# Operand b22 at the beginning of the FFN: when its high and low parts are made

## The chip, the core and the metric

The kernel runs on one core of a Trainium2 chip. Five engines work side by side and meet at semaphores: TensorE (PE, with its weight loads shown as PEld), VectorE (DVE), ScalarE (ACT), GpSimd (POOL) and SyncE (SP), which here issues nearly all DMAs. The metric is device time in microseconds for one execution of the whole block; the time of a kernel is the median of its runs.

## The reference

One decoder block on x (1 x 2048 x 1024): a mixer of eight stick-breaking attention heads and four pooling groups, and then a SwiGLU FFN of width 2816. Both have an RMSNorm ahead and behind, and are modulated from a vector c. What matters here is the passage from the mixer to the FFN:

```python
mix = jnp.concatenate([attn, pool], axis=-1) @ w_out[l]
x = x + gate_m * rmsnorm(mix, g_mix_post[l])

h = rmsnorm(x, g_ffn_pre[l]) * (1.0 + scale_f) + shift_f
f = (jax.nn.silu(h @ w_gate[l]) * (h @ w_up[l])) @ w_down[l]
x = x + gate_f * rmsnorm(f, g_ffn_post[l])
```

All is float32.

## The kernel before

**Products of float32.** Each operand of a product is split into a high part, rounded to the format that TensorE multiplies (a cast on ScalarE, line 59), and a low part, the rest (a subtraction on VectorE, line 60, which reads the source and the high part). `mm3` (lines 69 to 71) then makes three matmuls: high by high, low by high, high by low. `put(ops, n, cols, src)` (line 1156) is this split for 128 columns of a named operand.

**The FFN's products.** The 2048 tokens are taken in two halves of 1024. In each half the gate and up products are made as 2 x 2 block products with seven multiplications instead of eight. The token side has seven operands, b11, b21, t2, t3, t1, t4 and b22, sums and differences of quarters of h transposed (128 partitions x 4 x 512, a high and a low tile each). The weight side has a11, a12, s2, s3, s1, a22 and s4, made for each pair of 128-column blocks of a weight matrix by sums on GpSimd (lines 1267 to 1278). One *step* is one such product: four chunks of the inner dimension times three matmuls, twelve matmuls of 128x128 by 128x512, into one PSUM bank. For the first block of weights (j = 0 of the first half) the steps of the gate (g) and of the up matrix (u) are interleaved by `gate_up`:

- steps 0, 1: g with b11, b21; steps 2, 3: u with b11, b21
- steps 4, 5: g with t2, t3; steps 6, 7: u with t2, t3
- steps 8, 9, 10: g with t1, t4, b22; steps 11, 12, 13: u with t1, t4, b22
- from step 14 on: the next block of weights, seven g steps and then seven u steps

**PSUM.** Banks come from `f_ps` (line 1031), a cycle of eight tags with one buffer each. A step takes one, and so does each half of a row that is transposed (`modulated_t`, the tile `f_pt`). Results leave their bank by the functions a step has in `take`, which run one step later: `take_p1` copies it on ScalarE (line 1287), `plus` adds it to an earlier one on VectorE (line 1282, tiles `u2`, `u3`, `u4`), and `take_gate` adds it and applies Silu (lines 1331, 1332).

**The order around the beginning of the FFN.** The order of TensorE, ScalarE, VectorE and GpSimd is the order of the calls in the program. SP's is made by the compiler's planner: a DMA is put in when its tile's slot is free. The main loop (from line 1801) does for each step n: the functions due ahead of it, the step's matmuls, `end_of_rows(n)`, `split_up_to(n)` (which splits the weights up to five steps ahead), and then the takes due and a piece of a side job. At the beginning of the FFN three things stand beside the steps:

- the last row block of the mixer (its 128 tokens, `SEQUENCE[-1]`): `add_last_x` (line 1207) adds x in `split_up_to(0)`, `ffn_rows` (line 1193) squares and sums it on ScalarE after the step 0, `end_of_rows(1)` scales it (`x1s`, lines 1201 and 1202), and `put_h2` transposes, modulates and stores it;
- the late operands. t1, t4 and b22 have their room only once the mixer's tiles are closed. Their raw rows lie in DRAM and are loaded by `load` (line 1410) into twelve slots borrowed from other tags (`tr`, `gs`, `u4`, `s`); b22 takes the four slots of `tr`. All twelve loads are issued before step 0;
- `puts` (line 1413), a generator, splits them: one stretch between two `yield`s with each call of `next_side`.

Before the change `puts` runs through this list, where a number is one `put` (0 to 3 are the columns of b22, 4 to 7 of t1, 8 to 11 of t4) and None is the end of a stretch:

```python
for m in (0, 1, None, None, 4, 5, 6, 7, None, 8, 9, 10, 11, None, 2, 3, None):
```

So b22's first two columns are split in step 0, t1 in step 2, t4 in step 3, b22's other two columns in step 4, and the last row is put in step 5. In step 2 the side job runs ahead of the takes (the first gate sum, step 1's), in the others behind them.

Of the kernel before, what the change touches and what calls it, by code (L numbers as in the profile page):

```python
# [12 lines left out]
ALU = mybir.AluOpType  # L13
# [4 lines left out]
P = 128  # L18
# [3 lines left out]
HK = KC // 2  # L22
# [22 lines left out]
def block_kernel(ctx, tc, x, c, w_cond, b_cond, g_mix_pre, g_mix_post, w_in, w_pool,  # L45
                 pool_scale, w_out, g_ffn_pre, g_ffn_post, w_gate, w_up, w_down, out):
    nc = tc.nc
# [6 lines left out]
    def raw(ap):  # L54
        return ap.bitcast(F32)

    def split(hi, lo, src, low=nc.vector):

        nc.scalar.copy(hi, src)  # L59
        low.tensor_tensor(lo, src, raw(hi), ALU.subtract)  # L60
# [12 lines left out]
    def open_pool(stack, name, bufs=1, side=None):  # L73
        kw = {"side": side} if side else {}
        return stack.enter_context(tc.tile_pool(name=name, bufs=bufs, reuse_waits="tile", **kw))
# [39 lines left out]
    def ft(tag, name, shape=(P, TB)):  # L115
        return fx.tile(list(shape), F32, tag=tag, bufs=FT[tag], name=name)

    def rstd_of(pool, ss, name):

        v = pool.tile([P, 1], F32, tag="rs_v", bufs=2, name=f"{name}_v")  # L120
        nc.vector.tensor_scalar(v, ss, 1.0 / D, EPS, ALU.mult, ALU.add)
        r = pool.tile([P, 1], F32, tag="rs_r", bufs=4, name=f"{name}_r")
        nc.gpsimd.tensor_tensor(r, v, mhalf, ALU.pow)
        return r
# [174 lines left out]
    def normed_rows(tb, j, xs=None):  # L299
        t0 = tb * TB + j * P  # L300
        xt = tokp.tile([P, D], F32, tag="xt", name=f"xt{tb}_{j}")
        ss = tokp.tile([P, 1], F32, tag="ss", name=f"ss{tb}_{j}")
        if xs is None:
            xs = tokp.tile([P, D], F32, tag="xs", name=f"xs{tb}_{j}")
            nc.sync.dma_start(xt, xf[t0:t0 + P, :])
            nc.scalar.activation(xs, xt, AF.Square, scale=1.0 / 32, accum_out=ss)
        else:
            nc.scalar.activation(xt, xs, AF.Square, scale=1.0 / 32, accum_out=ss)
            xt = xs
        r = tokp.tile([P, 1], F32, tag="rs_r", bufs=4, name=f"x{tb}_{j}_r")  # L310
        v = tokp.tile([P, 1], F32, tag="rs_v", bufs=2, name=f"x{tb}_{j}_v")
        nc.vector.tensor_scalar(v, ss, 1.0, EPS, ALU.mult, ALU.add)
        nc.gpsimd.tensor_tensor(r, v, mhalf, ALU.pow)
        if tb == 1:
            return lambda: nc.vector.tensor_scalar_mul(xs, xt, r)
        nc.vector.tensor_scalar_mul(xs, xt, r)
        return xs
# [240 lines left out]
    loaded = []  # L558
# [144 lines left out]
    last_scale = normed_rows(1, 3, early1[3])  # L703
# [325 lines left out]
    SEQUENCE = [sb * NT // 2 + half * 4 + i for sb in range(2) for i in range(4) for half in range(2)]  # L1029
# [55 lines left out]
    for n in range(len(steps) + OFF):  # L1085
# [4 lines left out]
        if n < len(steps):  # L1090
            u, i = steps[n]
# [19 lines left out]
        for pool, here in ((hb, not wo and taken >= HB_FREE), (ha, len(wo) == 4 and fill is None)):  # L1111
            if here:
                hi, lo = (pool.tile([P, 4, D], F32R, tag=tag, name=f"wo_{pool.name}{tag}")
                          for tag in ("hi", "lo"))
# [32 lines left out]
    def new_ops(pool, sb, names):  # L1147
        return {n: (pool.tile([P, HK, TB], F32R, tag=f"{n}h", bufs=1, name=f"{n}h{sb}"),
                    pool.tile([P, HK, TB], F32R, tag=f"{n}l", bufs=1, name=f"{n}l{sb}")) for n in names}
# [6 lines left out]
    def put(ops, n, cols, src, low=nc.vector):  # L1156
        split(ops[n][0][:, :, cols], ops[n][1][:, :, cols], src, low)

    h2st, b22st = ExitStack(), ExitStack()
    ops = new_ops(open_pool(h2st, "ops0"), 0, EARLY)  # L1160
# [6 lines left out]
    def after_mix(T):  # L1167

        pss = mixed.pop(T)
        if T == SEQUENCE[-1]:  # L1170
            xt = last_x[0]
        else:
            xt = op.tile([P, D], F32, tag="xt", name=f"xr{T}")
            nc.sync.dma_start(xt, xf[T * P:(T + 1) * P, :])
        ss = op.tile([P, 2], F32, tag="ss", name=f"mss{T}")
        x1 = op.tile([P, D], F32, tag="x1", name=f"x1_{T}")
        halves = [slice(nh * TB, (nh + 1) * TB) for nh in range(2)]
        for nh in range(2):
            nc.scalar.activation(x1[:, halves[nh]], pss[nh], AF.Square, accum_out=ss[:, nh:nh + 1])
        nc.vector.tensor_tensor(ss[:, 0:1], ss[:, 0:1], ss[:, 1:2], ALU.add)  # L1180
        r = rstd_of(op, ss[:, 0:1], f"mr{T}")
        for nh in range(2):
            nc.vector.scalar_tensor_tensor(x1[:, halves[nh]], pss[nh], r, gm[:, halves[nh]], ALU.mult, ALU.mult)
            if T != SEQUENCE[-1]:
                nc.gpsimd.tensor_tensor(x1[:, halves[nh]], x1[:, halves[nh]], xt[:, halves[nh]], ALU.add)
        if T != SEQUENCE[-1]:
            nc.sync.dma_start(x1d[T], x1)
        return xt, x1

    def ffn_rows(T, xt, x1):  # L1190

        s2 = op.tile([P, 1], F32, tag="s2", name=f"s2_{T}")
        nc.scalar.activation(xt, x1, AF.Square, accum_out=s2)
        r2 = rstd_of(op, s2, f"fr{T}")
        if T != SEQUENCE[-1]:
            nc.vector.tensor_scalar_mul(xt, x1, r2)
            return xt

        def scale():
            xs = ft("gf", f"x1s{T}", (P, D))  # L1200
            nc.vector.tensor_scalar_mul(xs[:, 0:TB], x1[:, 0:TB], r2)
            nc.scalar.mul(xs[:, TB:], x1[:, TB:], r2)
            return xs
        return scale
# [7 lines left out]
    def put_h2(T, xs, pool=None):  # L1212

        i, second = T % NTS % HK, T % NTS >= HK
        cols = slice(i * P, (i + 1) * P)
        for kcs, h32 in modulated_t(pool or op, f_ps, xs, mods["af"], mods["bf"], f"f{T}"):
            nc.sync.dma_start(h2d[T][:, kcs, :], h32)
            if T >= NTS:
                continue
            low_k = kcs.start == 0  # L1220
            if not second:
                n = "b11" if low_k else "b21"
                put(ops, n, cols, h32)
                held_rows[n] = h32
            elif low_k:
                held_rows["b12"] = h32
            else:
                t3, t2 = held_rows["b12"], held_rows["b11"]
                nc.vector.tensor_tensor(t3, h32, t3, ALU.subtract)
                put(ops, "t3", cols, t3)  # L1230
                nc.vector.tensor_tensor(t2, t3, t2, ALU.add)
                put(ops, "t2", cols, t2)
                for n, t in (("t1", h32), ("t4", held_rows["b21"])):
                    nc.gpsimd.tensor_tensor(t, t, t2, ALU.subtract)
                    nc.sync.dma_start(lated[n][i], t)
# [164 lines left out]
    def late_operands():  # L1400

        slots = ["tr"] * 4 + ["gs"] * 3 + ["u4"] + ["s"] * 4
        todo = [(n, i) for n in ("b22", "t1", "t4") for i in range(HK)]
        raw = []

        def load():
            if len(raw) < len(todo):
                n, i = todo[len(raw)]
                t = ft(slots[len(raw) % len(slots)], f"{n}{i}_raw", (P, HK, P))
                nc.sync.dma_start(t, lated[n][i] if n in lated else h2d[HK + i][:, HK:KC, :])  # L1410
                raw.append(t)

        def puts():
            for m in (0, 1, None, None, 4, 5, 6, 7, None, 8, 9, 10, 11, None, 2, 3, None):
                if m is None:
                    yield
                    continue
                n, i = todo[m]
                put(ops, n, slice(i * P, (i + 1) * P), raw[m])
            put_h2(*late.pop(0), fx)  # L1420
            yield

        for _ in slots:
            load()
        return puts
# [348 lines left out]
    last_rows, last_scale = after_mix(SEQUENCE[-1]), []  # L1774
# [10 lines left out]
    takes, side, slow = {}, None, []  # L1785
# [3 lines left out]
    def next_side():  # L1789

        nonlocal side
        if slow:
            if next(slow[0], 0) == 0:
                slow.pop()
        elif side is not None and (n < HF or n % 2) and next(side, 0) == 0:
            side = None

    for n, s in enumerate(steps):
        for do in ahead.get(n, []):
            do()  # L1800
        s.ps = s.mm()
        end_of_rows(n)
        split_up_to(n)
        if n == 0:
            last_scale.append(ffn_rows(SEQUENCE[-1], *last_rows))
        if n in sides:
            side = sides[n]()
        jobs = [lambda: [do() for do in takes.pop(n, [])], lambda: next_side()]
        for do in jobs[::-1] if n == 2 else jobs:
            do()  # L1810
        for k, do in s.take:
            takes.setdefault(n + k, []).append(do)
    for n in sorted(takes):
# [28 lines left out]
```

## Time and profile before

| what | value |
|---|---|
| time, median of 3 runs | 2255.8 us (2254.81 to 2256.67) |
| profiled execution, its own time | 2258.0 us |
| its span, first to last instruction | 2256.2 us |
| mean granted TensorE clock | 0.998 |
| TensorE busy | 2231.4 us (99%) |
| VectorE busy | 1624.0 us (72%) |
| ScalarE busy | 1166.6 us (52%) |
| GpSimd busy | 1273.2 us (56%) |

All rows come from one profiled execution, with times in us from the first instruction. A row of the timeline is: start, duration, engine, source line, operation, output <- inputs, shape and count; several instructions of one kind in sequence are merged into one row (x2, x4), whose duration goes from the first start to the last end. In brackets stands how long the engine was idle ahead of it and what it waited for, as inferred from semaphore events. Matmuls are pipelined: one is shown with 0.39 us, but the next starts 0.227 us later, so a step's length is read from starts. Line 59 is the high part of any operand and line 60 the low part; the names tell which (`g_s_h` is the high part of a gate weight sum, `g_a_h` of a gate quarter, `b22l` the low part of b22).

### The profile page before, as it was taken

What the parts mean: (1) busy time and instruction counts of PE and PEld (TensorE: products, weight loads), DVE (VectorE), ACT (ScalarE), POOL (GpSimd) and SP (SyncE); (2) the same over time, 40 slices, a digit from 0 to 9 for tenths busy, and PEclk for the clock granted to TensorE, in tenths of its full rate; (3) what the DMA queues carried; (4) which work ended last, traced back from release to release, by engine and by line L of the source; (5) the groups of instructions that cost most, each with busy time, mean ns of one, the idle gap of its engine ahead of it and who ended that gap; (6) DMA issues with size and microseconds to landing.
All of it is one profiled execution on the core that took longest, in us unless ns stands there. A gap on an engine that the chain in (4) does not pass through costs nothing.

```text
span 2256.2 us, 33256 instructions
## 1 busy us (share of the span) xinstructions
PE 2231.4 (99%) x10613; PEld 1845.8 (82%) x10613; DVE 1624.0 (72%) x2227; ACT 1166.6 (52%) x2425; POOL 1273.2 (56%) x1579
## 2 busy tenths in 40 slices
PE   8999999999999999999999999999999999999998
PEld 6888888888888888888888888788888888888887
DVE  7874599999999957666565656777866555655566
ACT  5435599898999944452232323455532323234444
POOL 1452277787779955546868687321677565651003
PEclk9999999999999999999999999999999999999999
DMA  9986876534443556665554545777853333328664
GB/s 316 338 278 213 283 203 182 153 107 114 123 121 104 164 179 218 219 212 162 159 164 159 164 159 195 266 234 239 259 169 122 94 117 94 112 89 293 219 188 149
DMA packets 323980, 413.55 MB, mean 183 GB/s; under 512 B 20630, under 2 KB 189146, under 8 KB 323676
## 3 DMA queue, kind: packets, MB, share of 16 engines
q1 hardware_dynamic: 319196, 408.81, 57.1%
q10 hardware_dynamic: 4608, 2.63, 0.4%
q8 instruction: 83, 1.36, 0.3%
q14 instruction: 93, 0.76, 0.1%
HBM read 282.90 MB, written 128.45 MB: 182 GB/s over the span
## 4 chain that ended last, share of the span: by engine, by line
PE 87%; DVE 6%; ACT 2%; POOL 2%; issue 2%; DMA 1%; SPq 0%; DVEq 0%; ACTq 0%; POOLq 0%
PE wt L961 4%; PE t_u L70 3%; PE t_u L69 3%; PE t_u L71 3%; PE t_g L70 3%; PE t_g L69 3%; PE t_g L71 3%; PE dn0p L70 3%; PE dn0p L71 3%; PE dn0p L69 3%; PE dn1p L70 3%; PE dn1p L69 3%; PE dn1p L71 3%; PE mix L71 3%; PE mix L69 3%; PE mix L70 3%
## 5 line engine op out<-in xcount | busy, mean ns | idle before, releaser
L950 POOL TENSOR_TENSOR w<-sg,pr 128x512 f32<-128x512 f32 (+2 forms) x320 | 307.2, 960 | 46.5 <-DVE pr L945 13.4
L1342 POOL TENSOR_TENSOR s<-s,cu 128x512 f32<-128x512 f32 x88 | 133.9, 1528 | 240.3 <-DVE cu L1341 145.8
L945 DVE TENSOR_TENSOR_SCAN pr<-pr,carry,begin 128x512 f32<-128x512 f32 x192 | 243.9, 1271 | 0.0
L929 ACT ACTIVATE sg<-z 128x512 f32<-128x512 f32 (+2 forms) x320 | 183.4, 573 | 50.8 <-PE z L927 40.4
L60 DVE TENSOR_TENSOR wtl<-wt,wth 128x512 fp32r<-128x512 f32 (+1 forms) x320 | 189.3, 592 | 18.0 <-ACT wth L59 15.9
L59 ACT CAST wth<-wt 128x512 fp32r<-128x512 f32 (+1 forms) x320 | 182.1, 570 | 12.1 <-PE wt L961 12.1
L931 ACT ACTIVATE pr<-z 128x512 f32<-128x512 f32 (+2 forms) x320 | 182.5, 570 | 0.0
L961 PE MATMUL wt<-ident,w 128*128 128x128 f32 x1088 | 172.6, 273 | 2.0 <-POOL pr L941 1.1
L60 DVE TENSOR_TENSOR u_s_l<-u_s,u_s_h 128x512 fp32r<-128x512 f32 x66 | 65.2, 987 | 150.1 <-ACT u_s_h L59 150.0
L961 PEld LDWEIGHTS wt<-ident,w 128*128 128x128 f32 x1088 | 134.1, 140 | 33.4 <-POOL pr L941 1.9
L1332 ACT ACTIVATE s<-s 128x512 f32<-128x512 f32 x88 | 55.7, 633 | 190.5 <-DVE s L1331 190.5
L976 PE MATMUL av<-wth,vt 128*128 128x512 f32 (+1 forms) x320 | 126.5, 395 | 0.9 <-ACT o L981 0.8
L60 DVE TENSOR_TENSOR u_a_l<-u,u_a_h 128x512 fp32r<-128x512 f32 x66 | 77.1, 1169 | 63.7 <-ACT u_a_h L59 63.7
L70 PE MATMUL dn0p<-w0p_l,g0p_h 128*128 128x512 f32 x308 | 120.3, 391 | 1.0 <-DVE w0p_l L60 1.0
L59 ACT CAST g_s_h<-g_s 128x512 fp32r<-128x512 f32 x66 | 39.5, 620 | 157.8 <-POOL g_s L1274 78.2
L977 PE MATMUL av<-wtl,vt 128*128 128x512 f32 (+1 forms) x320 | 118.0, 369 | 1.9 <-DVE wtl L60 1.6
L69 PE MATMUL dn0p<-w0p_h,g0p_h 128*128 128x512 f32 x308 | 119.8, 389 | 0.0
L71 PE MATMUL dn0p<-w0p_h,g0p_l 128*128 128x512 f32 x308 | 119.8, 389 | 0.0
L926 PE MATMUL z<-kt,qt 128*128 128x512 f32 (+2 forms) x320 | 118.7, 371 | 0.7 <-ACT pr L931 0.6
L927 PE MATMUL z<-kt,qt 128*128 128x512 f32 (+2 forms) x320 | 117.0, 366 | 0.0
L59 ACT CAST u_s_h<-u_s 128x512 fp32r<-128x512 f32 x66 | 38.6, 614 | 150.3 <-POOL u_s L1274 149.1
L69 PE MATMUL dn1p<-w1p_h,g1p_h 128*128 128x512 f32 x292 | 113.6, 389 | 0.0
(657 smaller groups left out, 7184.2 us busy)
## 6 DMA issues: line engine op xcount, KB each, us to landing
g<-in_w_gate_dram SPq DMA_DIRECT2D x42, 512.0 KB, 5.3
u<-in_w_up_dram SPq DMA_DIRECT2D x42, 512.0 KB, 4.2
wc<-in_w_cond_dram SPq DMA_DIRECT2D x32, 512.0 KB, 7.5
qt<-qd SPq DMA_DIRECT2D x64, 256.0 KB, 4.0
kt<-kd SPq DMA_DIRECT2D x96, 128.0 KB, 3.3
vt<-vd SPq DMA_DIRECT2D x48, 256.0 KB, 4.0
wd<-in_w_down_dram SPq DMA_DIRECT2D x44, 256.0 KB, 3.4
tdt<-wd SPq DMA_DIRECT2D x44, 256.0 KB, 2.0
```

Source lines behind the costliest of these rows:

```text
L59: nc.scalar.copy(hi, src)
L60: low.tensor_tensor(lo, src, raw(hi), ALU.subtract)
L69: nc.tensor.matmul(ps, lh, rh, start=first and i == 0, stop=False)
L70: nc.tensor.matmul(ps, lh, rl, start=False, stop=False)
L71: nc.tensor.matmul(ps, ll, rh, start=False, stop=last and i == n - 1)
L929: nc.scalar.activation(sg[:, 0:L], z[:, 0:L], AF.Sigmoid, scale=0.125)
L931: nc.scalar.activation(pr[:, 0:L], z[:, 0:L], AF.Sigmoid, scale=-0.125)
L945: nc.vector.tensor_tensor_scan(keys, keys, begin, carry, ALU.mult, ALU.bypass)
L950: nc.gpsimd.tensor_tensor(w[:, 0:L], sg[:, 0:L], pr[:, 1:L + 1], ALU.mult)
L961: nc.tensor.transpose(wt[:, i * P:(i + 1) * P], wss[u][i][:, b * P:(b + 1) * P], ident)
L976: nc.tensor.matmul(av[:, lo0:], vb, wh[:, lo0:], start=first, stop=False)
L1342: nc.gpsimd.tensor_tensor(s, s, u, ALU.mult)
```

## The change

The high and low parts of b22 are no longer made together. All four high parts (ScalarE casts) are made in step 0 by an additional call of the side job ahead of `ffn_rows`, that is ahead of the last row's square. The low parts of columns 0 and 1 (VectorE) follow behind `ffn_rows` in step 0, where they were. In step 2 the side job is called twice: ahead of the takes it splits t1 as before, and behind the takes, so behind the first gate sum, it makes the low parts of columns 2 and 3, which were made in step 4 together with their high parts. t4 (step 3) and the last row (step 5) stay. The list of raw tiles is renamed, so that `raw` is the function that casts an operand's type. The instructions are the same in number and kind; no DMA is added, removed or put elsewhere in the program.

```diff
-        raw = []
+        loaded = []
...
         def puts():
-            for m in (0, 1, None, None, 4, 5, 6, 7, None, 8, 9, 10, 11, None, 2, 3, None):
-                if m is None:
+            def b22(low, *cols):
+                for i in cols:
+                    hi, lo = (t[:, :, i * P:(i + 1) * P] for t in ops["b22"])
+                    if low:
+                        nc.vector.tensor_tensor(lo, loaded[i], raw(hi), ALU.subtract)
+                    else:
+                        nc.scalar.copy(hi, loaded[i])
+            b22(False, *range(HK))
+            yield
+            b22(True, 0, 1)
+            yield
+            yield
+            for n in ("t1", "t4"):
+                for m in range(HK):
+                    put(ops, n, slice(m * P, (m + 1) * P), loaded[todo.index((n, m))])
+                yield
+                if n == "t1":
+                    b22(True, 2, 3)
                     yield
-                    continue
-                n, i = todo[m]
-                put(ops, n, slice(i * P, (i + 1) * P), raw[m])
+            yield
             put_h2(*late.pop(0), fx)
             yield
...
         split_up_to(n)
-        if n == 0:
-            last_scale.append(ffn_rows(SEQUENCE[-1], *last_rows))
         if n in sides:
             side = sides[n]()
-        jobs = [lambda: [do() for do in takes.pop(n, [])], lambda: next_side()]
-        for do in jobs[::-1] if n == 2 else jobs:
+        if n == 0:
+            next(side)
+            last_scale.append(ffn_rows(SEQUENCE[-1], *last_rows))
+        if n == 2:
+            next_side()
+        for do in takes.pop(n, []):
             do()
+        next_side()
```

More of the change, by code (lines that the diff above doesn't have):

```diff
@@ L1403, in late_operands @@
         todo = [(n, i) for n in ("b22", "t1", "t4") for i in range(HK)]
-        raw = []
+        loaded = []
         def load():
-            if len(raw) < len(todo):
-                n, i = todo[len(raw)]
-                t = ft(slots[len(raw) % len(slots)], f"{n}{i}_raw", (P, HK, P))
+            if len(loaded) < len(todo):
+                n, i = todo[len(loaded)]
+                t = ft(slots[len(loaded) % len(slots)], f"{n}{i}_raw", (P, HK, P))
                 nc.sync.dma_start(t, lated[n][i] if n in lated else h2d[HK + i][:, HK:KC, :])
-                raw.append(t)
+                loaded.append(t)
         def puts():
-            for m in (0, 1, None, None, 4, 5, 6, 7, None, 8, 9, 10, 11, None, 2, 3, None):
-                if m is None:
+            def b22(low, *cols):
[16 more added lines that the diff above has]
+                    b22(True, 2, 3)
                     yield
-                    continue
-                n, i = todo[m]
-                put(ops, n, slice(i * P, (i + 1) * P), raw[m])
+            yield
             put_h2(*late.pop(0), fx)
```

## The prediction

> **What bounds the kernel now.** I read the page first: how much of the span each engine works, and the chain of work that ended last.
>
> ```profile
> span 2256.2 us, 33256 instructions
> PE 2231.4 (99%) x10613; PEld 1845.8 (82%) x10613; DVE 1624.0 (72%) x2227; ACT 1166.6 (52%) x2425; POOL 1273.2 (56%) x1579
> PE 87%; DVE 6%; ACT 2%; POOL 2%; issue 2%; DMA 1%; SPq 0%; DVEq 0%; ACTq 0%; POOLq 0%
> ```
>
> TensorE sets the end. The change adds and removes no instruction, so it can only give time by closing a gap of TensorE, or cost time by opening one. The second view is therefore that of TensorE's waits, over 984 to 1078 us, where the FFN begins (first row), and over the whole span (the second).
>
> ```profile
> PE b_g L69 <- ACT g_a_h L59: 1.2, 1, 1.2
> ...
> PE dn0p L70 <- DVE w0p_l L60: 1.0, 3, 0.4
> ```
>
> There is one wait in the stretch. Its size I take from the timeline of TensorE, by the first matmul of a step and of the next (steps 9, 10, 11, 12), with the last of step 9:
>
> ```profile
> 1011.92 0.39 PE L69 MATMUL t_g<-t4h,g_a_h 128*128 128x512 f32 x1
> ...
> 1014.41 0.39 PE L71 MATMUL t_g<-t4h,g_a_l 128*128 128x512 f32 x1
> 1015.97 0.47 PE L69 MATMUL b_g<-b22h,g_s_h 128*128 128x512 f32 x1 [1.17 <-ACT g_a_h L59]
> ...
> 1018.82 0.39 PE L69 MATMUL t_u<-t1h,u_s_h 128*128 128x512 f32 x1
> ...
> 1021.54 0.39 PE L69 MATMUL t_u<-t4h,u_a_h 128*128 128x512 f32 x1
> ```
>
> A step that waits for nothing takes 1021.54 - 1018.82 = 2.72 us. Steps 9 and 10 together take 1018.82 - 1011.92 = 6.90 instead of 5.44: the wait and the slower matmuls behind it cost **1.46 us**. That is all there is to win in this stretch.
>
> **What the wait is for.** The row names the cast g_a_h, but in the code that is the weight of step 14, which step 10 doesn't read. What step 10 needs is a bank. From step 4 on the cycle of eight hands out: steps 4 and 5, two transposes of the last row (made in step 5), steps 6, 7, 8 and 9. Step 10 is the ninth and gets step 4's bank back, which the sum u2g on VectorE has to read first. VectorE's timeline, from the first gate sum on:
>
> ```profile
> 1004.64 0.68 DVE L1331 TENSOR_TENSOR s<-b_g,p1g 128x512 f32<-128x512 f32 x1
> 1006.53 0.69 DVE L60 TENSOR_TENSOR g_s_l<-g,g_s_h 128x512 fp32r<-128x512 f32 x1 [1.21 <-ACT g_s_h L59]
> 1007.53 2.50 DVE L60 TENSOR_TENSOR t4l<-t_raw,t4h 128x512 fp32r<-128x512 f32 x4 [0.31 <-ACT t4h L59]
> 1009.95 0.68 DVE L60 TENSOR_TENSOR g_a_l<-g,g_a_h 128x512 fp32r<-128x512 f32 x1
> 1010.55 0.68 DVE L1341 TENSOR_TENSOR cu<-b_u,p1u 128x512 f32<-128x512 f32 x1
> 1011.15 2.38 DVE L60 TENSOR_TENSOR b22l<-b_raw,b22h 128x512 fp32r<-128x512 f32 x2
> 1013.46 1.76 DVE L60 TENSOR_TENSOR g_s_l<-g_s,g_s_h 128x512 fp32r<-128x512 f32 x1
> 1015.15 0.68 DVE L1282 TENSOR_TENSOR u2g<-t_g,p1g 128x512 f32<-128x512 f32 x1
> 1015.75 1.35 DVE L140 TENSOR_SCALAR f_h<-f_pt,af,bf 128x128 f32<-128x128 f32 x4
> 1017.03 0.67 DVE L60 TENSOR_TENSOR u_s_l<-u,u_s_h 128x512 fp32r<-128x512 f32 x1
> ```
>
> u2g ends at 1015.15 + 0.68 = 1015.83, and TensorE goes on at 1015.97. g_a_h ended within 0.02 us of it, which is why the wait is put down to it. VectorE has no gap from 1007.53 on, so it is its backlog that makes u2g late; and two of its rows are long for their kind, because GpSimd works beside them:
>
> ```profile
> 1011.38 1.61 POOL L1342 TENSOR_TENSOR s<-s,cu 128x512 f32<-128x512 f32 x1 [10.70 <-DVE cu L1341]
> 1012.95 1.73 POOL L1278 TENSOR_TENSOR u_s<-u,u_s 128x512 f32<-128x512 f32 x1
> ```
>
> A low part alone takes 0.67 to 0.69 us; the second b22l and g_s_l, which met these two, took about 1.77, and ended some 0.5 us after the GpSimd operation.
>
> **The change, part by part.** First, the four high parts ahead of the square. ScalarE's rows:
>
> ```profile
> 991.64 1.16 ACT L59 CAST g_s_h<-g_s 128x512 fp32r<-128x512 f32 x2
> 995.97 1.06 ACT L1193 ACTIVATE xr_last<-x 128x1024 f32<-128x1024 f32 x1 [3.17 <-DVE x L1207]
> ...
> 997.03 1.12 ACT L59 CAST b22h<-b_raw 128x512 fp32r<-128x512 f32 x2
> 999.35 0.72 ACT L1202 ACTIVATE x1s<-x,fr_r 128x512 f32<-128x512 f32 x1 [1.20 <-POOL fr_r L123]
> ...
> 1009.48 1.14 ACT L59 CAST b22h<-b_raw 128x512 fp32r<-128x512 f32 x2
> 1010.53 0.62 ACT L59 CAST g_s_h<-g_s 128x512 fp32r<-128x512 f32 x1
> ```
>
> ScalarE is idle 3.17 us ahead of the square, waiting for VectorE's sum of x. Four casts take 2 x 1.12 = 2.24 us. They need the raw rows, whose loads are already issued in the first part of the FFN:
>
> ```profile
> L1410 SPq DMA_DIRECT2D b_raw<-h2d x4: 413/426/447, 987.5 to 989.0; - x4
> ...
> DMA to landing us min/median/max: 4.4/4.5/4.6
> ```
>
> The last one lands at 989.0 + 4.6 = 993.6. The casts run from 992.8, the fourth (0.6 us) from 994.3 to 994.9, 1.0 us ahead of the square: cost **0**. Without that cover the square, the last row's scale and all behind them would be late by what the casts overrun. The two casts taken from 997.03 leave a gap ahead of x1s, which waits for GpSimd anyway: 0. The two taken from 1009.48 bring g_s_h and all behind it forward by 1.05 us. Queued behind the casts on ScalarE is the square alone, for which VectorE's fr_v waits.
>
> Second, the low parts of columns 0 and 1 stay behind fr_v: 0. Third, those of columns 2 and 3 go behind the first gate sum, at 1005.24. There GpSimd shows nothing until 1011.38, so I take the duration that the first two have, 1.28 us for two:
>
> ```profile
> 998.23 1.28 DVE L60 TENSOR_TENSOR b22l<-b_raw,b22h 128x512 fp32r<-128x512 f32 x2
> ```
>
> They end at 1006.5, in the gap of 1.21 us that VectorE has there while ScalarE does the Silu and the next high part. g_s_l begins at 1006.53 as before, or 0.05 late at worst, and t4l has 0.31 more to spare: **0**. If this cover were gone, 1.28 us would go to t4l, g_a_l and cu; cu ends at 1011.23 and step 9, which takes its bank, starts at 1011.92, so 0.7 of it would be free.
>
> Fourth, behind cu the 2.31 us of b22l (1011.15 to 1013.46) are gone. g_s_l starts at 1011.15, its high part being ready at 1010.1. The case is not in the trace, so from both sides: it starts ahead of GpSimd's 1011.38 as the first b22l did and takes 0.68, or it meets GpSimd and ends at 1013.5 as the second b22l did. Then u2g ends at 1012.4 or at 1014.1. Step 9's matmuls leave room for the next step at 1014.64, with its weight load a slot ahead at 1014.4; both ends are in time. I take the first, whose start is the same as in the row. The gain is 0 at least, 1.46 at most; I take **-1.46**.
>
> What is late next? Step 11 would start at 1017.36, and needs u_s_l and the bank that u3g frees. Behind u2g come f_h to 1013.7 and u_s_l, which now meets GpSimd's u_s and ends by the rows at about 1014.68 + 0.5 = 1015.2, u3g at 1015.9: 1.5 us to spare. With the late end of g_s_l, u_s_l falls into GpSimd's gap from 1014.68 on and u3g still ends near 1016.8. The two slots of `tr` come free at 1006.5 instead of 1013.5, so SP may issue two loads of the down weights earlier; nobody waits for them here.
>
> The Trainium skill speaks against this part in "SBUF — State Buffer", section "Who interferes with whom": a VectorE operation with two SBUF inputs and a GpSimd one that reads SBUF exclude each other, and the later one is blocked until the first is done. By that, u_s_l brought forward into GpSimd's sum has to begin again at its end, 1014.68 + 0.68 = 1015.4 (an estimate), and the start of step 11 would still hold; the two long rows agree with it.
>
> **The sum:** 0 + 0 + 0 - 1.46. Of the profiled span that is 2256.2 - 1.46 = 2254.7; the profiled execution's own time is 2258.0, 2.2 above the median of the three runs, and all the change happens inside the span, so the median goes from 2255.8 to **2254.3**.
>
> **The rivals.** *Nothing gained* (2255.8): the wait is on ScalarE as the row says, or comes back at step 11. g_a_h stands behind u_s_h and this behind GpSimd's u_s, which starts from cu, and cu does not move; then TensorE would again start at 1015.97. For it speaks only the row, against it the code, where step 10 reads nothing of step 14. *More than the gap*: VectorE runs 2.3 us and more ahead, and the three waits for w0p_l, 1.0 us in all, go as well: 2255.8 - 2.46 = 2253.3. They lie in the down products, far behind this stretch, so the lead hardly lasts till there.
>
> *Slower*: VectorE's casts now fall into GpSimd's operations, and this makes the chain late that leads to step 23, the second block's first u product with t2. Its rows:
>
> ```profile
> 1031.31 1.28 POOL L1342 TENSOR_TENSOR s<-s,cu 128x512 f32<-128x512 f32 x1 [8.79 <-DVE cu L1341]
> ...
> 1046.55 1.29 POOL L1274 TENSOR_TENSOR u_s<-u,u 128x512 f32<-128x512 f32 x1
> ...
> 1048.53 1.11 DVE L60 TENSOR_TENSOR u_s_l<-u_s,u_s_h 128x512 fp32r<-128x512 f32 x1 [6.59 <-ACT u_s_h L59]
> ...
> 1051.91 0.39 PE L71 MATMUL t_u<-t2h,u_s_l 128*128 128x512 f32 x1
> ```
>
> GpSimd has hardly a gap from 1031.31 to 1047.84, and u_s_l ends at 1049.64, 2.2 us ahead of the matmul that reads it. With TensorE 1.46 earlier, some 0.7 is left. A new meeting costs a cast 1.77 - 0.68 = 1.1 us; VectorE has seven low parts between 1013 and 1030. If all seven met GpSimd anew, VectorE would lose 7.7 against a lead of 2.3, the chain would be 5.4 late, and the time 2255.8 - 1.46 + 5.4 - 0.7 = 2259.0. Slower than before begins at a slip of 2.2, that is above four new meetings. Against it: GpSimd works only about half of that stretch, and several of the seven are long already (u_a_l at 1018.23 takes 1.44 in the same timeline).
>
> ```profile
> 1018.23 1.44 DVE L60 TENSOR_TENSOR u_a_l<-u,u_a_h 128x512 fp32r<-128x512 f32 x1
> ```
>
> **How the numbers follow.** The forecast 0.74, nothing gained 0.16, more than the gap 0.05, slower 0.05. The forecast is that of the likeliest, 2254.3. The range takes in nothing gained and the larger gain, with half of the 1.9 us over which the three runs spread on either side: 2253.3 - 0.9 = 2252.4 to 2255.8 + 0.9 = 2256.7; only the slower case is left out. A measurement of this kernel can tell about 0.2%, 4.5 us, from no change. No case reaches it as worked out: the larger gain is 2.5, the worst of the slower case 3.2. So faster has 0.02 of the larger gain's 0.05 and slower 0.04 of the slower case's 0.05, should these be larger than their rows say; SP's order, which the planner makes anew, is in the latter. The rest, 0.94, is no change.
>
> **What would show it.** Right: b22h as four casts between 992.8 and 995, the square still at 995.97; two b22l between 1005.2 and 1006.5, g_s_l still at 1006.5; u2g ended by 1014.2; step 10 started 2.72 us after step 9, and no wait of TensorE in the stretch. Wrong: step 10 waits with u2g long done (then the wait was another's), the square later than 996.0 (a load landed late), or a wait at step 11 or 23.

## The result, and the profile after

| | before | changed |
|---|---|---|
| median | 2256.66 us (22 runs, 2254.81 to 2259.32) | 2253.06 us (22 runs, 2252.26 to 2254.84) |
| profiled execution, own time and span | 2258.0, 2256.2 us | 2253.0, 2251.2 us |

The ratio is 0.9985, with a 95% interval from 0.9978 to 0.9991: 3.6 us less, within the 0.2% that were called no change, and inside the range of the prediction, but more than twice the 1.46 us that it named as all there was to win in this stretch. Three pictures of the changed kernel's profile answer to those of before. First the page's span, busy times and chain:

```profile
span 2251.2 us, 33255 instructions
PE 2228.2 (99%) x10613; PEld 1844.4 (82%) x10613; DVE 1625.5 (72%) x2227; ACT 1167.6 (52%) x2425; POOL 1268.8 (56%) x1579
PE 89%; DVE 4%; ACT 2%; issue 2%; DMA 1%; POOL 1%; SPq 0%; DVEq 0%; ACTq 0%; POOLq 0%
```

Then TensorE's timeline: the first matmul of step 9, the last of it, the first of step 10 and of step 11.

```profile
1010.25 0.39 PE L69 MATMUL t_g<-t4h,g_a_h 128*128 128x512 f32 x1
...
1012.75 0.39 PE L71 MATMUL t_g<-t4h,g_a_l 128*128 128x512 f32 x1
1012.97 0.39 PE L69 MATMUL b_g<-b22h,g_s_h 128*128 128x512 f32 x1
...
1015.69 0.39 PE L69 MATMUL t_u<-t1h,u_s_h 128*128 128x512 f32 x1
```

Steps 9 and 10 take 1015.69 - 1010.25 = 5.44 us, without a wait. TensorE's waits from 984 to 1440 us are none at all now, so the three at the beginning of the down products are gone as well. Then ScalarE and VectorE, as far as the change moved their work:

```profile
991.04 2.22 ACT L1420 CAST b22h<-b_raw 128x512 fp32r<-128x512 f32 x4
994.31 1.06 ACT L1193 ACTIVATE xr_last<-x 128x1024 f32<-128x1024 f32 x1 [1.05 <-DVE x L1207]
```

```profile
1002.97 0.69 DVE L1331 TENSOR_TENSOR s<-b_g,p1g 128x512 f32<-128x512 f32 x1
1003.57 1.28 DVE L1418 TENSOR_TENSOR b22l<-b_raw,b22h 128x512 fp32r<-128x512 f32 x2
1004.87 0.69 DVE L60 TENSOR_TENSOR g_s_l<-g,g_s_h 128x512 fp32r<-128x512 f32 x1
...
1008.89 0.68 DVE L1341 TENSOR_TENSOR cu<-b_u,p1u 128x512 f32<-128x512 f32 x1
1009.49 0.68 DVE L60 TENSOR_TENSOR g_s_l<-g_s,g_s_h 128x512 fp32r<-128x512 f32 x1
1010.09 0.68 DVE L1282 TENSOR_TENSOR u2g<-t_g,p1g 128x512 f32<-128x512 f32 x1
```

The four high parts fill 2.22 of the gap of 3.17 us ahead of the square, which still waits for VectorE alone. The two low parts take 1.28 behind the gate sum. g_s_l follows cu at once, and u2g ends at 1010.77, 2.2 us before step 10 starts.

**Where the time went, matmul by matmul.** Both profiles have the same 10613 matmuls in the same order, so they can be compared one by one. The changed kernel is 1.63 us ahead after the first 52 us, in which the programs are the same; another 1.46 at step 11; another 2.08 by 1431 us of before; and 0.25 of that is lost near 1636 us, where a product with b22 waits 0.17. The first number is scatter between executions, from TensorE's slower first matmuls: the same matmul takes 0.63 in before and 0.39 in the changed kernel, and the granted clock from 50 to 52 us is 0.53 and 1.00.

```profile
51.06 0.63 PE L661 MATMUL first<-hth,wk_h 128*128 128x512 f32 x1
```

```profile
49.82 0.39 PE L661 MATMUL first<-hth,wk_h 128*128 128x512 f32 x1
```

Further profiles of both kernels (below) show that this number is not the change's: at 52 us a second one of before is 1.6 us ahead of the first too, and a second one of the changed kernel only 0.01. That one then wins 1.46 at step 11 and 2.08 by 1431 us, and ends 3.34 ahead. The change is thus worth 1.46 + 2.08 - 0.25 = 3.3 us; the 3.6 between the medians agrees with it within the interval.

The 2.08 has to be explained. The down products begin with these rows of before, TensorE and then VectorE:

```profile
1413.84 0.50 PE L70 MATMUL dn0p<-w0p_l,g0p_h 128*128 128x512 f32 x1 [0.24 <-DVE w0p_l L60]
1420.14 0.50 PE L70 MATMUL dn0p<-w0p_l,g0p_h 128*128 128x512 f32 x1 [0.39 <-DVE w0p_l L60]
1423.55 0.50 PE L70 MATMUL dn0p<-w0p_l,g0p_h 128*128 128x512 f32 x1 [0.39 <-DVE w0p_l L60]
```

```profile
1412.01 1.77 DVE L60 TENSOR_TENSOR w0p_l<-w0p,w0p_h 128x512 fp32r<-128x512 f32 x1
1413.71 0.68 DVE L1341 TENSOR_TENSOR cu<-b_u,u4u 128x512 f32<-128x512 f32 x1
1414.31 0.68 DVE L60 TENSOR_TENSOR g0p_l<-g0p,g0p_h 128x512 fp32r<-128x512 f32 x1
1414.91 1.78 DVE L60 TENSOR_TENSOR w0p_l<-w0p,w0p_h 128x512 fp32r<-128x512 f32 x1
...
1421.72 1.78 DVE L60 TENSOR_TENSOR w0p_l<-w0p,w0p_h 128x512 fp32r<-128x512 f32 x1
```

Here GpSimd still makes the last products and sums of the gate and up stage. One of its rows:

```profile
1421.33 1.62 POOL L1352 TENSOR_TENSOR gs<-s,gs 128x512 f32<-128x512 f32 x1
```

Seven low parts beside them, from 1412.01 to 1425.2, take 1.77 or 1.78 instead of 0.68 us, and two low parts are needed for each 2.72 us of TensorE. VectorE falls behind; how far it may fall depends on how far ahead it comes in. In the changed kernel seven low parts meet GpSimd there just the same, and TensorE doesn't wait:

```profile
1416.00 1.78 DVE L60 TENSOR_TENSOR w0p_l<-w0p,w0p_h 128x512 fp32r<-128x512 f32 x1
```

**A lag.** To measure that, I take the time from a block's first matmul to the sum u4u of its up product. For the second and the last block (of eleven) and the down products, before and changed:

```profile
1026.98 0.39 PE L69 MATMUL b_g<-b11h,g_a_h 128*128 128x512 f32 x1
1069.61 0.68 DVE L1282 TENSOR_TENSOR u4u<-t_u,u2u 128x512 f32<-128x512 f32 x1
...
1369.69 0.39 PE L69 MATMUL b_g<-b11h,g_a_h 128*128 128x512 f32 x1
1410.02 0.68 DVE L1282 TENSOR_TENSOR u4u<-t_u,u2u 128x512 f32<-128x512 f32 x1
1431.62 0.39 PE L69 MATMUL dn0p<-w0p_h,g0p_h 128*128 128x512 f32 x1
```

```profile
1023.85 0.39 PE L69 MATMUL b_g<-b11h,g_a_h 128*128 128x512 f32 x1
1063.91 0.68 DVE L1282 TENSOR_TENSOR u4u<-t_u,u2u 128x512 f32<-128x512 f32 x1
...
1366.57 0.39 PE L69 MATMUL b_g<-b11h,g_a_h 128*128 128x512 f32 x1
1404.30 0.68 DVE L1282 TENSOR_TENSOR u4u<-t_u,u2u 128x512 f32<-128x512 f32 x1
1426.41 0.39 PE L69 MATMUL dn0p<-w0p_h,g0p_h 128*128 128x512 f32 x1
```

In the second block the lag is 42.6 before and 40.1 changed, in the last 40.3 and 37.7. The difference is 2.6 us at both ends: over nine blocks VectorE, ScalarE and GpSimd keep the whole lead. They run at a pace of their own: from one block's u4u to the next it is 37.85 us in both kernels (but for the last two, about 38.6 and 36.9), while TensorE takes 38.08 for a block. So the lag shrinks by 0.23 a block in both, and the difference between them stays. In before none of the three waits for TensorE from 1065 to 1400 us; in the changed kernel, with the lead, ScalarE does five times (4.1 us in all, ahead of casts g_a_h), and the pace is the same. From the last block's first matmul to the last row shown TensorE takes 61.9 before and 59.8 changed: 2.1 us lost and nothing.

### The profile page after: what moved, and what is told of

Read it like the earlier page. It is cut to its first block, busy times and chain, and to the rows that moved or that the text cites. A ratio compares the mean times of both kernels' runs of the same rounds, so it can differ in the third digit from the quotient of the medians.

```text
span 2251.2 us, 33255 instructions
## 1 busy us (share of the span) xinstructions
PE 2228.2 (99%) x10613; PEld 1844.4 (82%) x10613; DVE 1625.5 (72%) x2227; ACT 1167.6 (52%) x2425; POOL 1268.8 (56%) x1579
## 3 DMA queue, kind: packets, MB, share of 16 engines
q8 instruction: 83, 1.36, 0.2%
## 4 chain that ended last, share of the span: by engine, by line
PE 89%; DVE 4%; ACT 2%; issue 2%; DMA 1%; POOL 1%; SPq 0%; DVEq 0%; ACTq 0%; POOLq 0%
PE wt L961 4%; PE t_u L69 4%; PE t_u L71 4%; PE t_u L70 4%; PE t_g L71 3%; PE t_g L69 3%; PE t_g L70 3%; PE dn1p L70 3%; PE dn1p L69 3%; PE dn1p L71 3%; PE b_u L69 3%; PE b_u L71 3%; PE b_u L70 3%; PE dn0p L70 3%; PE dn0p L69 3%; PE dn0p L71 3%
## 5 line engine op out<-in xcount | busy, mean ns | idle before, releaser
L59 ACT CAST u_s_h<-u_s 128x512 fp32r<-128x512 f32 x66 | 38.6, 614 | 150.8 <-POOL u_s L1274 149.0
```

## The experiments

The ratio is to the kernel before, timed beside each on the same chip. Steps 9 and 10, the lag in the last block and the time lost (what TensorE takes from that block's first matmul to the row shown above, less 59.84 us) are read from each one's profile in the same way.

| kernel | steps 9, 10 | GpSimd's first product | lag | lost | ratio (95%) |
|---|---|---|---|---|---|
| before | 6.90 | 1.61 | 40.32 | 2.08 | |
| before, second profile | 6.93 | 1.60 | 40.31 | 2.09 | |
| before, third profile | 6.93 | 1.61 | 41.69 | 3.45 | |
| high parts alone | 6.94 | 1.61 | 40.88 | 2.65 | 1.0000 (0.9991 to 1.0009) |
| high parts behind the square | 5.44 | 1.61 | 37.05 | 0 | 0.9988 (0.9979 to 0.9997) |
| before, u2g first | 5.44 | 2.21 | 39.60 | 1.36 | 1.0000 (0.9991 to 1.0009) |
| changed, 4 repeats | 5.44 | 1.61 | 41.03 | 2.78 | 1.0001 (0.9993 to 1.0010) |
| changed, 2 repeats | 5.44 | 1.62 | 39.31 | 1.09 | 0.9990 (0.9980 to 0.9999) |
| before, 4 repeats | 5.44 | 2.82 | 41.57 | 3.34 | 1.0013 (1.0004 to 1.0023) |
| before, no last sums | 5.44 | 2.82 | 40.40 | 0.84 | 0.9994 (0.9984 to 1.0004) |
| changed | 5.44 | 1.61 | 37.73 | 0 | 0.9985 (0.9978 to 0.9991) |
| changed, second profile | 5.44 | 1.61 | 37.45 | 0 | |

**The high parts alone.**

```diff
                 if n == "t1":
-                    b22(True, 2, 3)
                     yield
+            b22(True, 2, 3)
             yield
             put_h2(*late.pop(0), fx)
```

> The change's first part alone: all four high parts of b22 ahead of the square, all low parts where they were before (columns 2 and 3 behind cu in step 4). Theory (VectorE's low parts decide): nothing gained. u2g ends 1.2 us after step 9's matmuls have left room, so steps 9 and 10 together take 6.9 us as before, VectorE's lead in the later blocks is that of the kernel before, and the three waits at the beginning of the down products (1413 to 1424 us) stay; ratio to before 1.000, +-0.0005. Rival (ScalarE's two casts less ahead of the wait decide): steps 9 and 10 take 5.44 us, ratio 0.9985.

Measured: ratio 1.0000, steps 9 and 10 at 6.94. The waits at the down products stay too, with 2.65 lost; that it is more than before's 2.08 goes with a wait of 2.0 us for a down weight's high part that VectorE has in the last block. Moving ScalarE's casts gives nothing.

**The high parts behind the square.**

```diff
-            b22(False, *range(HK))
             yield
+            b22(False, *range(HK))
             b22(True, 0, 1)
```

> The change's other part alone: the low parts of columns 2 and 3 behind the first gate sum as in the changed kernel, but the four high parts together behind the last row's square, in the gap that ScalarE has there. Theory: the whole gain, ratio 0.9985; steps 9 and 10 take 5.44 us and no wait at the beginning of the down products. ScalarE ends the four casts about 0.1 us ahead of x1s, so up to 0.1 us late is possible there. Rival (ahead of the square is needed): x1s and all behind it late, a wait at step 8, 9 or 10, ratio above 0.9995.

The ratio is 0.9988, which agrees with the changed kernel's 0.9985 within the intervals, and TensorE has no wait from 984 to 1440 us. ScalarE's rows of this kernel:

```profile
994.30 1.06 ACT L1193 ACTIVATE xr_last<-x 128x1024 f32<-128x1024 f32 x1 [3.17 <-DVE x L1207]
...
995.36 2.17 ACT L1420 CAST b22h<-b_raw 128x512 fp32r<-128x512 f32 x4
997.68 0.73 ACT L1202 ACTIVATE x1s<-x,fr_r 128x512 f32<-128x512 f32 x1 [0.16 <-POOL fr_r L123]
```

The casts end at 997.53 and x1s waits for GpSimd all the same. That the high parts come ahead of the square has no share in the gain, and that all four are made in step 0 has one only in so far as columns 2 and 3 are ready for their low parts; the place of these low parts decides.

**Step 4's sum ahead of step 10's split.**

```diff
         end_of_rows(n)
+        if n == 5:
+            for do in takes.pop(n, []):
+                do()
         split_up_to(n)
```

> The kernel before with one sum put earlier: in step 5 the sum u2g, which empties step 4's bank, is made ahead of the low part g_s_l of step 10's weight and not behind it. Theory (step 10 waits for the bank): u2g ends near 1014.1 us in the times of before, step 10's first two matmuls start 2.72 us after step 9's, and only its third waits, for g_s_l, to about 1015.3; steps 9 and 10 take about 6.2 us instead of 6.9. Rival (step 10 waits for the cast g_a_h, which the row names, behind GpSimd's sum): step 10's first matmul starts 4.05 us after step 9's as before. The waits at the down products stay by both, since VectorE makes the same work; ratio 0.9995 to 1.000.

Measured: no wait at step 10, not even of its third matmul. The experiment is not a clean one, since something else had changed as well, as VectorE's rows show:

```profile
1010.33 1.28 DVE L60 TENSOR_TENSOR b22l<-b_raw,b22h 128x512 fp32r<-128x512 f32 x2
1011.53 0.69 DVE L1282 TENSOR_TENSOR u2g<-t_g,p1g 128x512 f32<-128x512 f32 x1
1012.13 1.19 DVE L60 TENSOR_TENSOR g_s_l<-g_s,g_s_h 128x512 fp32r<-128x512 f32 x1
```

The two b22l took 1.28 and not 2.38, ahead of the edit, and GpSimd's product 2.21 and not 1.61: here VectorE came first where GpSimd had before.

**The changed kernel, held up later.** The low part of one weight sum of the second block is made again, with the same result.

```diff
                 split(h, l, st[w])
+                if (kind, sb, j, w) == ("g", 0, 1, "s2"):
+                    for _ in range(4):
+                        nc.vector.tensor_tensor(l, st[w], raw(h), ALU.subtract)
```

> The changed kernel with VectorE held up later: the low part of one weight sum of the second block (step 16) is made five times instead of once, with the same result, 4 x 0.6 = 2.4 us more on VectorE where TensorE waits for nothing. Theory (the gain at the down products is the lead that VectorE won at the FFN's beginning and kept over ten blocks): steps 9 and 10 take 5.44 us as in the changed kernel, VectorE, ScalarE and GpSimd run 2.4 us later from the second block on, and the three waits at the beginning of the down products come back, about 2.1 us; ratio to before 0.9993. Rival (the waits there went for another reason, SP's order or chance): no waits there, ratio 0.9985.

VectorE's row and TensorE's waits from 984 to 1440 us:

```profile
1024.09 2.87 DVE L1305 TENSOR_TENSOR g_s_l<-g_s,g_s_h 128x512 fp32r<-128x512 f32 x4
```

```profile
PE dn0p L70 <- DVE w0p_l L60: 1.7, 3, 0.9
```

Steps 9 and 10 keep their 5.44, and the three waits are back, 390 us behind the repeats. They cost more than forecast: the lag is 41.0, higher than before's, and 2.78 are lost. The gain at the down products hangs on the lead.

**Half of it.** The same with `range(2)`.

> The changed kernel with half of that hold-up: the low part of step 16's weight is made three times instead of once, 1.2 us more on VectorE. The lag of the side engines is read from the sum u4u of the first half's last block, after that block's first matmul: 40.3 us before, 41.0 with four repeats, 39.6 with u2g ahead, 37.7 changed; the time lost at the beginning of the down products was 2.1, 2.8, 1.4 and 0 us. Theory (lost time = lag - 38.25, not below 0): lag 38.9, 0.7 us lost there, one wait of TensorE or two. Rival (the loss does not follow the lag but falls out by chance): none lost or two and more.

The lag is 39.31, 0.4 more than expected, and 1.09 are lost, in one wait. By the rule written down ahead of it, 39.31 - 38.25 = 1.06.

**The kernel before, held up.** The same four repeats in the kernel before.

> The kernel before with the low part of step 16's weight made five times, 2.4 us more on VectorE. Theory (lost time = lag - 38.25): lag 42.7, so 4.5 us lost at the beginning of the down products, 2.4 more than before; steps 9 and 10 take 6.9 us; ratio 1.001. Rival (the side engines catch up in the ten blocks between): lag 40.3 and the time of before.

The side engines don't catch up, and the ratio is 1.0013. Against the forecast, step 10 did not wait in this run (below), and the lag is 41.57 and not 42.7. That is 1.2 over the run without last sums (40.40, next), whose code is the same up to here and where step 10 did not wait either: the repeats take 2.9 here too, but a low part g_a_l ahead of them, which met GpSimd there and took 1.75, takes 0.68; what moved GpSimd there was not followed up. The rule gives 3.32; 3.34 are lost, 0.68 of them ahead of the down products, at the last block's first u product with t2.

**GpSimd's last sums left out.** For the last block of the first half, s1 to s4 of gate times up are not made, and a product is stored in their place, so this kernel's result is another.

```diff
-                    nc.gpsimd.tensor_tensor(t, x, y, op)
-                    keep(n, t)
+                    if sb == 0 and j == HF - 1:
+                        keep(n, s)
+                    else:
+                        nc.gpsimd.tensor_tensor(t, x, y, op)
+                        keep(n, t)
```

> The kernel before without GpSimd's four sums of the last block of the first half (s1 to s4 of its gate times up; a product is stored in their place), which stand from 1416 to 1423 us beside the first low parts of the down products. Theory (VectorE falls behind there because seven of its low parts meet GpSimd and take 1.77 instead of 0.68 us): the low parts from 1416.6 on take 0.68, the second and third wait of TensorE there go (1420 and 1423.5), the first (1413.8, beside GpSimd's products) stays; some 1.3 us less than before. Rival (they wait for loads, or VectorE's amount of work alone is the cause): the three waits stay.

At before's lag, 40.40, only 0.84 are lost instead of the rule's 2.15: 1.31 less, as expected. VectorE's rows and TensorE's only wait:

```profile
1413.98 1.78 DVE L60 TENSOR_TENSOR g0p_l<-g0p,g0p_h 128x512 fp32r<-128x512 f32 x1
1415.68 0.68 DVE L60 TENSOR_TENSOR w0p_l<-w0p,w0p_h 128x512 fp32r<-128x512 f32 x1
1416.28 0.68 DVE L60 TENSOR_TENSOR g0p_l<-g0p,g0p_h 128x512 fp32r<-128x512 f32 x1
```

```profile
1411.21 0.50 PE L70 MATMUL dn0p<-w0p_l,g0p_h 128*128 128x512 f32 x1 [0.32 <-DVE w0p_l L60]
```

The low parts are short as soon as GpSimd has nothing beside them. What sets the loss is this meeting, entered with too small a lead.

**Both kernels profiled again.** In the last two runs, whose code up to step 10 is that of before, step 10 did not wait. So I asked whether before always waits.

> The kernel before, unchanged, profiled again. In two of the runs so far whose code is that of before up to step 10, VectorE's second low part of b22 met GpSimd's first product and waited for it, and step 10 waited; in two others VectorE went first, GpSimd's product took 2.8 us in place of 1.6, and step 10 did not wait. Theory (the order of the two is decided anew in each execution): over this profile and the next, steps 9 and 10 take 6.9 us exactly where that product takes 1.6, and 5.4 where it takes 2.8; in both cases the last block's lag is about 40.3 and about 2 us are lost at the down products. Rival (the code of those two runs made the difference): 6.9 us in both profiles.

> The kernel before, unchanged, profiled a third time, with the same two cases and by each theory the same numbers as in the second profile of it.

> The changed kernel, unchanged, profiled again. Theory: no low part of b22 stands beside GpSimd's first product any more, so there is no such choice; steps 9 and 10 take 5.44 us, the last block's lag is 37 to 38 and nothing is lost at the down products. Rival (the gains were one execution's): a wait at step 10 or at the down products.

Before waited at step 10 in both (6.93), with GpSimd's product at 1.60 and 1.61; the changed kernel waited in neither of its profiles. So the wait goes with the product's length, as the theory says; that it falls out anew in each execution of one and the same program was not seen, and the rival stands. The times of single executions leave it open. The eleven of the high parts alone fall into two groups, four from 2252.6 to 2253.6 and seven from 2255.8 to 2258.3; but the first 52 us scatter by up to 1.7, so this doesn't show which executions waited. The third profile has a lag of 41.69 and 3.45 lost (the rule: 3.44), because VectorE waited 2.5 us there for a high part that waited for a load of down weights. This and the first 52 us may be part of why before's own runs spread by 4.5 us.

## Why the prediction was right, and where it was not

**The wait at step 10** went as worked out: 1.46 forecast, 6.90 - 5.44 = 1.46 measured; the high parts cost nothing, the low parts took 1.28 in the gap of 1.21, and of the two ends of g_s_l the one I took came, with u2g 1.2 us behind cu. That the wait was for u2g's bank and not for g_a_h, which the row names, was argued from the code. The held-up kernel of before shows that it was not g_a_h: TensorE starts step 10 well ahead of that cast.

```profile
1014.42 0.39 PE L69 MATMUL b_g<-b22h,g_s_h 128*128 128x512 f32 x1
```

```profile
1015.84 0.62 ACT L59 CAST g_a_h<-g 128x512 fp32r<-128x512 f32 x1
```

In all eight profiles without the wait step 10 starts ahead of that cast. The bank itself is not shown by a clean experiment; that step 10 starts 0.15 us behind the end of u2g in all four profiles that wait (in the run with the high parts alone 1014.93 + 0.68 = 1015.61, step 10 at 1015.76) fits it.

**The step that failed** is "They lie in the down products, far behind this stretch, so the lead hardly lasts till there." The lead lasted whole, 2.6 us over nine blocks, and the rival that I gave 0.05 came true. I had the evidence unread: in before's waits from 1065 to 1400 us VectorE, ScalarE and GpSimd wait for one another in every row but two, one for a load and one without a releaser. Here the group of engines that the bound engine does not stop kept its head start.

**Its price was mis-sized too.** I took 1.0 us for the three waits from the view of waits, and 2.08 were lost. That view counts the idle time of TensorE between modelled ends; from starts a wait costs more, as I had worked out for step 10 (1.17 in the row, 1.46 from starts), and I did not do the same for these. With 1.46 + 2.08 the forecast would have been 2255.8 - 3.5 = 2252.3.

**Luck.** That the median lies inside the range is luck in part. The forecast starts from before's median of three runs, 2255.8; over 22 runs it was 2256.66. With the measured gain of 3.6 from that start, 2252.2, the changed kernel would lie just below the range's end at 2252.4.

**The other rivals.** Nothing gained: refuted by both profiles of the changed kernel. Slower: the meetings it feared are few. Of the low parts between cu and the next block's, the longest take 1.80 and 1.17, and the place where they would have cost time, the u product with t2, lost it only in the kernel before with four repeats (0.68 us, in the last block). The order of SP changed only by two stores put ahead of one load, without a cost.

## What to carry to other kernels

Where one engine sets the end and the others run beside it at a pace of their own, time saved on the others is not lost for lack of a wait nearby: look for the next place, however far, where they fall behind, and measure by a lag whether the lead gets there. Price a wait from the starts of the instructions around it, not from the idle time in the row. And where operations of two engines hold each other up and start close together, look at which of the two goes first, in more than one profile.

## What was not expected of the hardware

Two operations on VectorE and GpSimd that meet can fall out either way by a hair. In before and in its kernel with four repeats, the same instructions stand there, and GpSimd's product starts 0.83 us behind cu in both (1011.38 - 1010.55 and 1011.21 - 1010.38). In the one VectorE's two b22l took 2.38 and the product 1.61; in the other:

```profile
1010.99 1.28 DVE L60 TENSOR_TENSOR b22l<-b_raw,b22h 128x512 fp32r<-128x512 f32 x2
```

```profile
1011.21 2.82 POOL L1345 TENSOR_TENSOR s<-s,cu 128x512 f32<-128x512 f32 x1 [10.71 <-DVE cu L1344]
```

An operation of this kind takes 1.28 alone (the row at 1031.31 in the prediction), so by an estimate it got going near 1012.75: behind the second b22l, which ended at 1012.27, and about when VectorE came to u2g (1012.79), which reads one input from PSUM. In the run with u2g first it is 1012.77 - 1.28 = 1011.49, and u2g starts at 1011.53. GpSimd waited through more than one low part. The Trainium skill, "SBUF — State Buffer", section "Who interferes with whom", says that the order of issue decides who is blocked. The traces agree for the first b22l, which starts ahead of the product in both kernels and goes first. They differ for the second in the kernel with four repeats: by the rows it starts at 1011.59, 0.38 us behind the product, and is done first, in 0.69 us. Four profiles of code that is the same here fell out for GpSimd and three for VectorE; what tips it is open. The blocked low parts ended 0.55 us after GpSimd's operation and not a full 0.68, so the estimate drawn from that page in the prediction was a little late: in the changed kernel u_s_l ended 0.55 us behind GpSimd's sum (1011.96 + 1.17 against 1011.28 + 1.30).
